# A two-layer encoder trunk on one core: feed-forward tiles in twos, transposes in longer runs, another job order

## The chip, the cores and the metric

The kernel runs on one core of a Trainium2 chip. The metric is the device time of one execution in microseconds (us). The kernel before took 728.59 us, the median of three runs (728.37 to 728.87).

A core has TensorE (matrix products, written to eight PSUM banks), VectorE, ScalarE and GpSimd (elementwise work), and SyncE, whose queue issues the transfers from memory. In the profile these are PE (its weight loads are PEld), DVE, ACT, POOL and SP.

## The reference

The input is one sequence of 256 positions, 1024 wide. Each of the two layers does, with float32 weights:

```python
ada = c_act @ w_ada[l] + b_ada[l]            # six vectors of 1024: shift, scale, gate, twice
h = rms(x, g_mix[l]) * (1.0 + sc1) + sh1
parts = split(h @ w_in[l])                    # queries, keys, values, two gates
y_a = gqa_attention(qa, ka, va) @ w_branch_a[l]      # 8 query heads, 2 key heads, 256 keys
y_b = dilated_attention(qs, kss, vs) @ w_branch_b[l] # 3 groups of 4 heads, strided windows
x = x + gt1 * ((sigmoid(ga) * y_a + sigmoid(gb) * y_b) @ w_out[l])
h2 = rms(x, g_mlp[l]) * (1.0 + sc2) + sh2
x = x + gt2 * (square(relu(h2 @ w_ff1[l])) @ w_ff2[l])   # 1024 -> 4096 -> 1024
```

Queries and keys are normalized and rotated before the attention.

## The kernel before

**Two-part numbers.** A large product is computed from operands split into a high part and a low remainder, each in the reduced float32 format that TensorE takes in one pass. A weight tile (128 x 1024, 512 KB) is loaded to a buffer `wr`; ScalarE copies it into the high half of a buffer `w`, and VectorE subtracts to make the low half (`split_next`). A product then is three passes: high by high, low by high, high by low (`mm3`, `many`).

**The first feed-forward layer.** The 4096 hidden columns are taken in eight rounds j of 512. Round 0 (`ff1_first`) has its own form. In rounds 1 to 7, `ff1(j)` handles four tiles of 128 columns, two for each half u. For a tile, `two_sums` runs eight *wide* passes: the tile's high half is the stationary operand, and the high and low parts of the activations stream through side by side, 512 columns, into one PSUM bank. Then eight *narrow* passes follow, with the tile's low half and the activations' high part, 256 columns, added to the bank's first half. ScalarE and VectorE add the bank's halves, apply the squared ReLU and split the result. Between two rounds stand the passes of the second feed-forward layer for the round before: four weight tiles of twelve wide passes each.

**Transposes.** Normalized activations, queries, keys, mixed values and attention probabilities are transposed on TensorE, 128 x 128 at a time, as `pe.transpose` against the identity (in the profile a MATMUL with `xin`, which holds the identity, and 128 columns), and copied out of PSUM by ScalarE or VectorE. In `att_a_soft`, for one step j of the grouped attention, the two key heads g come one after the other: maximum (VectorE), two exponentials with sums (ScalarE), reciprocal, two scalings (ScalarE), four transposes into a bank, a copy out.

**Order.** No engine's order is written by hand. Every operation is recorded (`Plan.record`; all instructions therefore carry line 676, where they are issued) with an estimated occupancy and latency. `Plan.due` gives each a due time, working back from TensorE's order, and `Plan.run` then plays the program forward in time: on each engine that is free, the ready operation with the earliest due time goes next, if a buffer or bank for its result can be had (`fits`). This is done in four passes, each taking its due times from the starts of the one before, and the best of the four by its own clock is issued. For TensorE the planner knows a price for changing between products that use the whole array and those that use parts of it (`CUT`, by the `cut` of an operation); a transpose counts as whole, and changing to or from one is free in its account. `plan.together()` marks operations that must follow one another without anything between; the first of them then waits for what any of them needs.

**Jobs.** TensorE's first order, from which the due times start, is the order of recording. In the mixer of a layer it is the list `seq0` or `seq1` in `CFG`: `c2` to `c5` a block of the query, key and value projection, `u` and `v` half a gate block, `a` a step of the grouped attention, `b` a step of the dilated one, `y` a part of the branch projection, `w` one tile of the modulation vectors `ada` (a 512 KB load and one VectorE reduction of 128 x 1024, nothing on TensorE). `ada_f0` and `ada_f1` say how many such tiles follow each feed-forward round. The weight tiles are loaded by SP's queue in the order in which the jobs name them.

Of the kernel before, what the change touches and what calls it, by code (L numbers as in the profile page):

```python
# [20 lines left out]
P = 128  # L21
D = 1024
S = 256
# [3 lines left out]
KT = D // P  # L27
# [6 lines left out]
CFG = dict(ahead0=1,  # L34
  post0=(5, 2, 1, 0), s2k=9, ahead=1, last="k",
  hk=2,
  ada_f0=[1, 5, 6, 1, 1, 6, 1, 4, 2], ada_f1=[4, 0, 0, 0, 0, 2, 1, 0, 0],
  seq0="a v w v w w c4 c3 w w w v a a u u w w w v a w w w w w b w w w u w v w b w w y w y w y w y".split(),
  seq1="v w w a w u a w c4 w v c3 w w w w u c5 w w w u a w a c2 w y w y y u y b w w w w b v w w w v".split())
WR = 7  # L40
NB8 = 16
WARM = 5
# [3 lines left out]
BEGIN = 20000.0  # L46
# [15 lines left out]
    shift={})  # L62
COLD = 5200.0
FILL = (6000.0, 3), (8500.0, 4)
CUT = {"row": 290.0, "col": 240.0, "rowcol": 290.0, "": 125.0}
DEEP = 3
URGE = 500.0
GIVE = 0.75
# [73 lines left out]
def pattern(z):  # L142
    return z.ap if isinstance(z, View) else z if hasattr(z, "tensor") else None
# [10 lines left out]
class Plan:  # L154
# [101 lines left out]
    def record(self, e, op, a, k):  # L256
        outs = [k["out"]] if "out" in k else [a[0]]
        outs += [z for z in (k.get("accum_out"),) if z is not None]
        ins = [z for z in list(a if "out" in k else a[1:]) + [v for n, v in k.items() if n not in ("out", "accum_out")] if pattern(z) is not None]
        if op == "tensor_tensor_reduce":  # L260
            outs.append(ins.pop())
        o = dict(e=e, op=op, a=a, k=k, w=[self.foot(z) for z in outs], r=[self.foot(z) for z in ins], i=len(self.ops))
        o["also"], o["then"], o["soon"] = [], None, self.soon and e == "SP"
        o["from"] = self.earliest
        if self.group is not None:
            self.group.append(o)
        outs, ins = [pattern(z) for z in outs], [pattern(z) for z in ins]
        o["occ"], o["lat"] = self.cost(e, op, outs, ins, k)
        o["occ"] += self.hold
        o["cut"] = ""  # L270
        if e == "PE" and op == "matmul":
            o["cut"] = self.division(outs[0], ins[0])
        o["rush"] = self.urgent and e in ("DVE", "ACT")
        from_sbuf = all(z.space == bass.MemoryType.SB for z in ins)
        o["port"] = from_sbuf and op != "reciprocal" and k.get("op") != ALU.pow and "reduce" not in op.replace("tensor_tensor_reduce", "")
        self.ops.append(o)
# [145 lines left out]
    def run(self, due):  # L422
        ops = self.ops
        n = len(ops)
        left = [len(o["need"]) for o in ops]
        ready = [o["from"] for o in ops]
        start = [None] * n
# [5 lines left out]
        dve_port, held_port, last_cut = 0.0, (0.0, 0.0), ""  # L433
# [68 lines left out]
        def taken(i):  # L502
            z = 0.0
            for name in banks[i]:
                e, end = reader.get(name, (None, 0.0))
                if e != ops[i]["e"]:
                    z = max(z, end)
            return z
# [5 lines left out]
        t = 0.0  # L514
        count = 0
        while count < n:
            moved = False
            for e in ORDERED:
                if free[e] > t:
                    continue  # L520
                w, q = wait[e], now[e]
                if then[e] is not None:
                    pick = then[e]
# [4 lines left out]
                else:  # L528
                    pick = None
                while w and w[0][0] <= t:  # L530
                    i = heapq.heappop(w)[1]
# [6 lines left out]
                held = []  # L538
                forced = pick is not None
                while q and not forced:  # L540
                    d, i = heapq.heappop(q)
                    z = taken(i)
                    if z > t:
                        heapq.heappush(ev, (z, 0, -1))
                        if e not in again:
                            again.append(e)
                    elif fits(i):
                        pick = i
                        break
                    held.append((d, i))  # L550
                    if len(held) > 40:
                        break
                if pick is None:
                    seen[e] = state[0]
                if pick is not None and e != "SP" and not forced:

                    end = t + ops[pick]["occ"]
                    for r, j in w:
                        if r < end and due[j] < due[pick] - self.patience and (r - t) < 0.5 * ops[pick]["occ"] and fits(j):
                            held.append((due[pick], pick))  # L560
                            pick = None
                            break
                    if pick is not None and rushed[e] and not ops[pick]["rush"] and called(e, pick, end):
                        held.append((due[pick], pick))
                        pick = None
# [9 lines left out]
                o = ops[pick]  # L575
                then[e] = o["then"]
                start[pick] = t
                slow = 0.0
                if e == "PE":
                    cut = o["cut"]  # L580
                    if cut != last_cut:
                        slow = CUT[cut]
                    last_cut = cut
                    if t < COLD and o["occ"] < 1000.0:
                        slow += o["occ"]
                if e == "DVE" and o["port"]:
                    if held_port[0] <= t < held_port[1]:
                        slow = held_port[1] - t
                    dve_port = t + o["occ"] + slow
                elif e == "POOL" and not o["port"]:  # L590
                    slow = max(0.0, dve_port - t - 80.0)
                elif e == "POOL" and o["port"]:

                    slow = max(0.0, dve_port - t - 80.0)
# [3 lines left out]
                if e == "SP":  # L598
                    quiet = t < 4000.0
                    b = max(pipe[0], t + (1200.0 if t < 4000.0 else 2100.0)) + o["lat"] / RATE[t < 50000.0]  # L600
# [29 lines left out]
            t = max(t, ev[0][0])  # L630
            while ev and ev[0][0] <= t:
                _, kind, i = heapq.heappop(ev)
# [47 lines left out]
def encoder(ctx: ExitStack, tc: tile.TileContext, a: dict, out: bass.AP):  # L680
# [4 lines left out]
    plan = Plan(tc, dict(sbuf=pool_of("ap"), psum=pool_of("pp", space=PSUM)))  # L685
    act, dve, pool, pe, sp = plan.lanes()
    tl = plan.tile

    def pa(name):
        return tl("psum", [P, 512], F32, "ps", 8, name)  # L690
# [4 lines left out]
    def pt(name):  # L695
        return tl("psum", [P, 512], F32, "ps", 8, name)
# [10 lines left out]
    ident, small, gc = xin[:, :P], xin[:, P : 2 * P], xin[:, 2 * P : 2 * P + 8]  # L707
# [102 lines left out]
    def weights(n=None):  # L810
        while todo and len(ready) < (n or CFG["ahead"]):
            split_next()
        return ready.pop(0)

    def weights_k(k):
        return [z.rearrange("p (k n) -> p k n", k=k) for z in weights()]
# [259 lines left out]
    def keep_pt(ps, o):  # L1076
        act.activation(o, ps, AF.Copy)
        return o
# [15 lines left out]

    def att_a_soft(l, j, sps, home):

        pts = []
        for g in range(2):
            nm = f"a{l}_{g}_{j}"
            sv = sps[j, g].rearrange("p (t n) -> p t n", t=2)  # L1100
            st = tl("sbuf", [P, 3, 2], F32, "st", 6, f"st{nm}")
            dve.tensor_reduce(out=st[:, 0, :], in_=sv, op=ALU.max, axis=AX.X, negate=True)
            pr = tl("sbuf", [P, 2, S], F32, "pr", 4, f"pr{nm}")
            for t in range(2):
                act.activation(
                    pr[:, t, :], sv[:, t, :], AF.Exp, bias=st[:, 0, t : t + 1], accum_out=st[:, 1, t : t + 1]
                )
            dve.reciprocal(st[:, 2, :], st[:, 1, :])
            for t in range(2):
                scale_p(pr[:, t, :], st[:, 2, t : t + 1], PSCALE[l])  # L1110
            tp = pt(f"t{nm}")
            for kt in range(2):
                for t in range(2):
                    pe.transpose(
                        tp[:, kt * S + t * P : kt * S + (t + 1) * P], pr[:, t, kt * P : (kt + 1) * P], ident
                    )
            pts.append(keep_pt(tp, home[:, 2 * (j % 2) + g]))
        return pts

    def att_a_out(l, T, j, pts, ops):  # L1120

# [105 lines left out]

    def two_sums(ps, wh, wl, xs, nk):  # L1230

        for k in range(nk):
            pe.matmul(ps, wh[:, k, :], xs.both(k).rearrange("p u n -> p (u n)"), start=k == 0, stop=False)
        for k in range(nk):
            pe.matmul(ps[:, :S], wl[:, k, :], xs.both(k)[:, 0], start=False, stop=k == nk - 1)

    fl = lambda z: z.rearrange("p a b -> p (a b)")

# [136 lines left out]
    def mlp(l, h2):  # L1375
# [42 lines left out]
        def ff1(j):  # L1418
            hid = hid_tiles(j)
            for u in range(2):  # L1420
                r = s2k(f"r{l}_{j}_{u}")
                for i in range(2):
                    wh, wl = weights_k(KT)
                    ps = pa(f"f{l}_{j}_{u}{i}")
                    two_sums(ps, wh, wl, h2, KT)
                    ri = r[:, i * S : (i + 1) * S]
                    act.activation(ri, ps[:, S:], AF.Copy)
                    dve.tensor_tensor(ri, ps[:, :S], ri, op=ALU.add)
                act.activation(r, r, AF.Relu)
                act.activation(r, r, AF.Square)  # L1430
                split_hid(r, *hid[u])
            return hid
# [17 lines left out]
        for j in range(1, 8):  # L1450
            hids.append(ff1(j))
            ada(ffn_ada[j])
            if j < 7:
                for i in range(4):
                    w = weights()
# [4 lines left out]
        ws = []  # L1460
# [47 lines left out]
        for c0 in halves:  # L1508
            cs = slice(c0, c0 + 256)
            acc = pb(f"gated{c0}")[:, :256]  # L1510
            for q, (j, i, w) in enumerate(ws[6:]):
                wh, wl = (gated[:, q, z, c0 - 512 : c0 - 256] for z in range(2))
# [21 lines left out]
    c_row, pick = c_in[:, :P], c_in[:, P:]  # L1534
# [102 lines left out]
    pss = {c: [pb(f"q0_{c}_{t}") for t in range(2)] for c in (0, 1, 2, 5)}  # L1637
# [42 lines left out]
    for k in range(1, KT):  # L1680
        ada(2)
        v = shg[0, 0]
# [5 lines left out]
        for pair in ((0, 1), (2, 5)) if k < KT - 1 else ((2, 5), (0, 1)):  # L1688
            w = weights(CFG["ahead0"])
            jobs = []  # L1690
            for t in range(2):
                for i, c in enumerate(pair):
                    wh, wl = (z[:, i * 512 : (i + 1) * 512] for z in w)
# [10 lines left out]
    h2 = mixer(0, hT, T)  # L1704
# [8 lines left out]
    ws = []  # L1713
    for t in range(2):
        pss = [pb(f"q1_{c}_{t}") for c in range(2)]
        for k in range(KT):
            if t == 0:
                ws.append(weights())
            for c in range(2):
                lh, ll = hT.parts(k, slice(t * P, (t + 1) * P))  # L1720
                wh, wl = (z[:, c * 512 : (c + 1) * 512] for z in ws[k])
# [3 lines left out]
    h2 = mixer(1, hT, T)  # L1725
# [99 lines left out]
```

## Time and profile before

| | |
|---|---|
| median of three runs | 728.59 us (728.37 to 728.87) |
| the profiled execution's own time | 728.5 us |
| its span, first to last instruction | 726.7 us |
| PE busy | 721.3 us, 99%, 3844 matmuls |
| DVE, ACT, POOL busy | 584.1, 467.0, 64.9 us |
| moved by DMA | 180.95 MB, mean 249 GB/s |
| granted TensorE clock | 1.00 |

Matmuls are pipelined, and the length that the profile gives one (some 0.39 us for a wide pass) runs on while the next has begun. The pace is read from one start to the next. In the timeline view neighbouring instructions of one kind form a row: its start, the time to the end of its last, what it is, and how many; what it writes stands ahead of `<-` and what it reads behind it. A transpose between wide passes splits a row of them.

### The profile page before, as it was taken

The page shows a single profiled execution, that of the slowest core. Times are in us where ns is not written, and L with a number is a line of the kernel's source. Part 1 is how long each engine was busy: PE and PEld are TensorE (multiplying, and loading weights), DVE is VectorE, ACT ScalarE, POOL GpSimd, SP SyncE. Part 2 cuts the span into 40 slices and gives each one's busy share as a digit, 9 for nine tenths or more (in the row PEclk, how much of TensorE's full clock was granted, in tenths as well). Part 3 has the DMA queues.
Part 4 walks back from the last instruction along what each step waited for, and adds up shares of the span by engine and source line. Part 5 has one row for each costly group of instructions (what it writes and reads, how often), then busy time and mean ns, then how long its engine had stood idle before and what let it go on. Part 6 is the DMA issues. An engine that isn't in the chain of part 4 may idle for free.

```text
span 726.7 us, 10619 instructions
## 1 busy us (share of the span) xinstructions
PE 721.3 (99%) x3844; PEld 599.1 (82%) x3844; DVE 584.1 (80%) x911; ACT 467.0 (64%) x791; POOL 64.9 (9%) x60
## 2 busy tenths in 40 slices
PE   9999999999999999999999999999999999999998
PEld 7787887788888888888887888778888888888887
DVE  6999999999999878683799788797889965566543
ACT  6669679875657765663475946858846856556540
POOL 1007540000000050000003011010000000000000
PEclk9999999999999999999999999999999999999999
DMA  8997669996499988684556777858456965686201
GB/s 350 407 406 246 203 202 326 355 356 211 144 343 400 380 321 308 252 298 146 203 161 225 246 276 262 297 175 285 142 207 217 379 242 172 210 286 179 83 0 59
DMA packets 50868, 180.95 MB, mean 249 GB/s; under 512 B 5728, under 2 KB 6784, under 8 KB 50816
## 3 DMA queue, kind: packets, MB, share of 16 engines
q1 hardware_dynamic: 50816, 180.28, 70.6%
q8 instruction: 30, 0.49, 0.3%
q14 instruction: 22, 0.18, 0.1%
HBM read 178.66 MB, written 1.06 MB: 247 GB/s over the span
## 4 chain that ended last, share of the span: by engine, by line
PE 96%; ACT 1%; DVE 1%; DMA 1%; issue 0%; POOL 0%; SPq 0%; DVEq 0%
PE ps L676 96%; DMA xin<-in_x 1%; ACT pr L676 0%; ACT s2k L676 0%; ACT w L676 0%; DVE s2k L676 0%; POOL ss L676 0%; DVE w L676 0%; ACT v L676 0%; DVE st L676 0%; DVE xin L676 0%; SPq L676 0%; DVE ss L676 0%; DVEq L676 0%; DVE shg L676 0%
## 5 line engine op out<-in xcount | busy, mean ns | idle before, releaser
L676 DVE TENSOR_TENSOR w<-wr,w 128x1024 fp32r<-128x1024 f32 x234 | 281.4, 1224 | 43.4 <-ACT w L676 42.5
L676 ACT ACTIVATE w<-wr 128x1024 fp32r<-128x1024 f32 x234 | 240.4, 1058 | 60.7 <-PE ps L676 39.2
L676 PE MATMUL ps<-w,hT 128*128 128x512 f32 x1032 | 250.3, 396 | 0.2 <-DVE s2k L676 0.2
L676 PEld LDWEIGHTS ps<-w,hT 128*128 128x128 f32 x1032 | 190.1, 188 | 41.6 <-issue 1.4
L676 PE MATMUL ps<-w,hid 128*128 128x512 f32 (+1 forms) x780 | 176.0, 385 | 0.0
L676 PEld LDWEIGHTS ps<-w,hid 128*128 128x128 f32 x780 | 143.1, 188 | 28.3
L676 PE MATMUL ps<-hT,w 128*128 128x256 f32 (+1 forms) x896 | 159.1, 337 | 0.0
L676 PEld LDWEIGHTS ps<-hT,w 128*128 128x128 f32 x896 | 139.2, 189 | 19.3
L676 DVE CUSTOM_DVE_ANT_0 s2k<-wr,c_act 128x1024 bf16<-128x1024 f32 x96 | 116.6, 1222 | 4.5 <-DMA wr<-in_w_ada 4.5
L676 ACT ACTIVATE s2k<-ps 128x256 f32<-128x256 f32 (+3 forms) x108 | 44.8, 444 | 78.3 <-PE ps L676 78.1
L676 PE MATMUL ps<-w,mT 128*128 128x512 f32 x192 | 45.7, 393 | 0.0
L676 DVE TENSOR_TENSOR s2k<-ps,s2k 128x256 f32<-128x256 f32 x56 | 23.1, 419 | 26.0 <-ACT s2k L676 25.9
L676 ACT ACTIVATE s2k<-s2k 128x512 f32<-128x512 f32 (+1 forms) x62 | 38.5, 623 | 8.3 <-DVE s2k L676 7.4
L676 PEld LDWEIGHTS ps<-w,mT 128*128 128x128 f32 x192 | 35.5, 188 | 7.2 <-DVE mT L676 0.2
L676 POOL TENSOR_TENSOR rstd<-rstd,half 128x8 f32<-128x8 f32 (+1 forms) x20 | 31.0, 1554 | 100.0 <-DVE rstd L676 99.7
L676 DVE TENSOR_TENSOR hid<-s2k,hid 128x512 fp32r<-128x512 f32 x28 | 19.2, 689 | 24.1 <-ACT hid L676 24.0
L676 ACT ACTIVATE pr<-pr,st 128x256 f32<-128x256 f32 (+1 forms) x64 | 32.7, 563 | 2.7 <-DVE st L676 2.7
L676 POOL TENSOR_TENSOR ss<-ss,half 128x1 f32<-128x1 f32 x8 | 5.8, 730 | 257.4 <-DVE ss L676 257.4
L676 PE MATMUL ps<-xin,s2k 128*128 128x128 f32 x180 | 26.9, 273 | 0.7 <-ACT s2k L676 0.7
L676 PEld LDWEIGHTS ps<-xin,s2k 128*128 128x128 f32 x180 | 21.7, 140 | 6.9 <-ACT s2k L676 1.4
L676 PE MATMUL ps<-w,oa 128*128 128x512 f32 x96 | 24.0, 397 | 0.0
L676 DVE TENSOR_TENSOR s2k<-ps,gtb 128x512 f32<-128x512 f32 (+1 forms) x18 | 11.7, 658 | 15.0 <-PE ps L676 15.0
(106 smaller groups left out, 508.0 us busy)
## 6 DMA issues: line engine op xcount, KB each, us to landing
wr<-in_w_ff SPq DMA_DIRECT2D x120, 512.0 KB, 5.0
wr<-in_w_ada SPq DMA_DIRECT2D x96, 512.0 KB, 5.3
wr<-in_w_gate SPq DMA_DIRECT2D x32, 512.0 KB, 5.4
wr<-in_w_qkv SPq DMA_DIRECT2D x24, 512.0 KB, 4.9
wr<-in_w_x SPq DMA_DIRECT2D x16, 512.0 KB, 5.6
wr<-in_w_out SPq DMA_DIRECT2D x16, 512.0 KB, 5.1
wr<-in_w_y SPq DMA_DIRECT2D x8, 512.0 KB, 6.5
wr<-in_w_ba SPq DMA_DIRECT2D x8, 512.0 KB, 6.1
```

Of the source, the lines that this page charges most:

```text
L676: getattr(self.real[o["e"]], o["op"])(*map(real, o["a"]), **{n: real(z) for n, z in o["k"].items()})
```

## The change

1. `two_sums` takes a list of banks and tiles. `ff1(j)` calls it once for each half u with both tiles: sixteen wide passes, then sixteen narrow ones, instead of eight and eight, twice. Both banks and both weight tiles are held until the end.
2. Transposes get a `cut` of their own, `"t"`: going to them is free in the planner's account, going back to a whole-array product costs 55 ns (`LEAVE`).
3. When TensorE's next operation by due time is of another kind than the last one, the planner looks among the 40 ready operations that are due first for one of the last kind: due at most 1000 ns later if the last was a transpose or used parts of the array (`LINGER`), 300 ns if it was an ordinary product (`SHY`). If there is one, it goes first. This holds from 20 us on.
4. `att_a_soft` records the softmax of both key heads first, and then the eight transposes into two banks under `plan.together()`, and the two copies behind them.
5. `seq0`, `seq1`, `ada_f0` and `ada_f1` have another order. Layer 0's list keeps the first jobs nearly as they are and moves the last gate job behind both dilated steps; layer 1's begins with a gate job and a projection block.

```diff
-  ada_f0=[1, 5, 6, 1, 1, 6, 1, 4, 2], ada_f1=[4, 0, 0, 0, 0, 2, 1, 0, 0],
-  seq0="a v w v w w c4 c3 w w w v a a u u w w w v a w w w w w b w w w u w v w b w w y w y w y w y".split(),
-  seq1="v w w a w u a w c4 w v c3 w w w w u c5 w w w u a w a c2 w y w y y u y b w w w w b v w w w v".split())
+  ada_f0=[3, 1, 8, 2, 1, 6, 2, 4, 2], ada_f1=[2, 0, 0, 0, 0, 0, 0, 0, 0],
+  seq0="w a v w v w w c3 c4 w w v a a w u u w w v a w w w w w b w v b w w w w w w w u y w y y y w w".split(),
+  seq1="u w c4 v a w w w w w u a c3 w v a c5 u w w w w w w c2 w a w y y y y u b b v v w w w w w w w v w".split())
...
-CUT = {"row": 290.0, "col": 240.0, "rowcol": 290.0, "": 125.0}
+CUT = {"row": 290.0, "col": 240.0, "rowcol": 290.0, "": 125.0, "t": 0.0}
+LEAVE = 55.0
+LINGER = 1000.0
+SHY = 300.0
...
+        if e == "PE" and op == "transpose":
+            o["cut"] = "t"
...
+                if e == "PE" and pick is not None and not forced and t > BEGIN and ops[pick]["cut"] != last_cut:
+                    more = LINGER if last_cut else SHY
+                    for d, i in sorted(q)[:40]:
+                        if d > due[pick] + more:
+                            break
+                        if ops[i]["cut"] == last_cut and fits(i):
+                            q.remove((d, i))
+                            heapq.heapify(q)
+                            held.append((due[pick], pick))
+                            pick = i
+                            break
...
-                        slow = CUT[cut]
+                        slow = LEAVE if last_cut == "t" and not cut else CUT[cut]
...
-            tp = pt(f"t{nm}")
-            for kt in range(2):
-                for t in range(2):
-                    pe.transpose(
-                        tp[:, kt * S + t * P : kt * S + (t + 1) * P], pr[:, t, kt * P : (kt + 1) * P], ident
-                    )
-            pts.append(keep_pt(tp, home[:, 2 * (j % 2) + g]))
-        return pts
+            prs.append(pr)
+        tps = [pt(f"ta{l}_{g}_{j}") for g in range(2)]
+        with plan.together():
+            for g in range(2):
+                for kt in range(2):
+                    for t in range(2):
+                        pe.transpose(
+                            tps[g][:, kt * S + t * P : kt * S + (t + 1) * P], prs[g][:, t, kt * P : (kt + 1) * P], ident
+                        )
+        return [keep_pt(tps[g], home[:, 2 * (j % 2) + g]) for g in range(2)]
...
-    def two_sums(ps, wh, wl, xs, nk):
-
-        for k in range(nk):
-            pe.matmul(ps, wh[:, k, :], xs.both(k).rearrange("p u n -> p (u n)"), start=k == 0, stop=False)
-        for k in range(nk):
-            pe.matmul(ps[:, :S], wl[:, k, :], xs.both(k)[:, 0], start=False, stop=k == nk - 1)
+    def two_sums(pss, ws, xs, nk):
+
+        for ps, (wh, _) in zip(pss, ws):
+            for k in range(nk):
+                pe.matmul(ps, wh[:, k, :], xs.both(k).rearrange("p u n -> p (u n)"), start=k == 0, stop=False)
+        for ps, (_, wl) in zip(pss, ws):
+            for k in range(nk):
+                pe.matmul(ps[:, :S], wl[:, k, :], xs.both(k)[:, 0], start=False, stop=k == nk - 1)
...
-                for i in range(2):
-                    wh, wl = weights_k(KT)
-                    ps = pa(f"f{l}_{j}_{u}{i}")
-                    two_sums(ps, wh, wl, h2, KT)
+                ws = [weights_k(KT) for _ in range(2)]
+                pss = [pa(f"f{l}_{j}_{u}{i}") for i in range(2)]
+                two_sums(pss, ws, h2, KT)
+                for i, ps in enumerate(pss):
```

More of the change, by code (lines that the diff above doesn't have):

```diff
@@ L36 @@
   hk=2,
-  ada_f0=[1, 5, 6, 1, 1, 6, 1, 4, 2], ada_f1=[4, 0, 0, 0, 0, 2, 1, 0, 0],
-  seq0="a v w v w w c4 c3 w w w v a a u u w w w v a w w w w w b w w w u w v w b w w y w y w y w y".split(),
-  seq1="v w w a w u a w c4 w v c3 w w w w u c5 w w w u a w a c2 w y w y y u y b w w w w b v w w w v".split())
+  ada_f0=[3, 1, 8, 2, 1, 6, 2, 4, 2], ada_f1=[2, 0, 0, 0, 0, 0, 0, 0, 0],
+  seq0="w a v w v w w c3 c4 w w v a a w u u w w v a w w w w w b w v b w w w w w w w u y w y y y w w".split(),
+  seq1="u w c4 v a w w w w w u a c3 w v a c5 u w w w w w w c2 w a w y y y y u b b v w w w w w w w w v w".split())
 WR = 7
@@ L1095, in att_a_soft @@
     def att_a_soft(l, j, sps, home):
-        pts = []
+        prs = []
         for g in range(2):
```

## The prediction

> **What bounds the kernel now.** I read the page's busy shares and slices first, then its waits, then TensorE's timeline piece by piece.
>
> ```profile
> PE 721.3 (99%) x3844; PEld 599.1 (82%) x3844; DVE 584.1 (80%) x911; ACT 467.0 (64%) x791; POOL 64.9 (9%) x60
> ...
> PEclk9999999999999999999999999999999999999999
> ```
>
> ```profile
> PEld ps L676 <- issue: 5.0, 17, 0.4
> PEld ps L676 <- ACT s2k L676: 2.3, 3, 0.9
> PEld ps L676 <- ACT pr L676: 1.4, 3, 0.7
> ...
> PEld ps L676 <- DVE w L676: 0.4, 1, 0.4
> ```
>
> TensorE is busy for 99% of the span at full clock, and nothing holds it long: its weight loads wait 5.0 us for issue and 2.3 us on the largest engine row. No matmul is added or removed. The gain can only come from what consecutive matmuls cost beyond their steady pace, and from the few waits. That pace is read from start to start in the timeline (columns: start us, length us, what, count).
>
> ```profile
> 246.31 11.31 PE L676 MATMUL ps<-hT,w 128*128 128x512 f32 x64
> 257.45 11.07 PE L676 MATMUL ps<-w,hid 128*128 128x512 f32 x48
> 268.36 11.31 PE L676 MATMUL ps<-hT,w 128*128 128x512 f32 x64
> ...
> 334.52 5.72 PE L676 MATMUL ps<-hT,w 128*128 128x512 f32 x32
> ...
> 701.35 20.82 PE L676 MATMUL ps<-w,hid 128*128 128x512 f32 x108
> 722.01 1.60 PE L676 MATMUL ps<-gated,hid 128*128 128x256 f32 x12
> ```
>
> ```profile
> L676 PE MATMUL ps<-gated,hid 128*128 128x256 f32 x12 | 1.6, 283 | 0.0
> ```
>
> One round of the feed-forward (one j) takes (334.52 − 246.31) / 4 = 22.053 us. By the code it holds 80 wide passes (32 in the x64, 48 in the x48) and 32 narrow ones, in 4 groups of 8 wide, 8 narrow. A narrow pass takes n = (1.60 − 0.283) / 11 = 0.120 us. The x108 piece holds 72 wide and 36 narrow and follows a narrow group. Let e be what it costs to go from narrow back to wide: 722.01 − 701.35 = 20.66 = 72 w + 36 n + e, and 22.053 = 80 w + 32 n + 4 e. These give w = 0.227 us and **e = 0.019 us**; reading errors of 0.01 us move e by some 0.005.
>
> **Part 1, tiles in twos.** Two tiles' wide passes run together, then their narrow ones: 28 groups per layer become 14, so over both layers 28 returns go, 28 × 0.019 = **−0.53 us**. It is on TensorE, so on the path. Unknown is whether the return costs more after 16 narrow passes than after 8. If it doubles, the gain is 0; if not, 0.53. I take 0.53, because inside a group the narrow passes keep their pace (the 12 at the end give the same 0.120), so nothing visible builds up. What moves besides: the second tile's high half is needed 8 narrow passes (0.96 us) earlier, and the first tile's low half 8 wide ones (1.8 us) later. Covers: the weights. The loads' waits above show one wait for a low half, 0.4 us, in the whole run, and this stage is where it would be tightest:
>
> ```profile
> 204.00:226.00 22.00, 22.00 (x114) 18.78 (x113) 21.62 (x34) 14.26 (x21) 0.00 (x0) 1.00 0.98 379
> 226.00:248.00 22.00, 22.00 (x114) 18.82 (x113) 21.88 (x29) 18.03 (x25) 0.00 (x0) 1.00 1.01 396
> ```
>
> ```profile
> ACT w L676 <- PE ps L676: 39.2, 25, 3.7
> ```
>
> VectorE is 98% to 99% busy and the DMA engines are full there (shares 0.98 and 1.01), yet TensorE never pauses; and the copies of the weights' high halves wait 39.2 us in all for TensorE to give back a buffer or a bank, so they are ahead of it. I cost it at nothing; were the lead gone, each of 28 pairs could lose up to 0.96 us. The results leave later: both banks of a pair are drained after its narrow passes, while the next pair writes two others; the 10.91 us of second-layer passes between rounds hide the rest.
>
> **Part 2, transposes in longer runs.** The transposes stand in some 75 runs behind the opening, from 64.06 to 679.17 us.
>
> ```profile
> 64.06 0.60 PE L676 MATMUL ps<-xin,s2k 128*128 128x128 f32 x4
> ...
> 170.99 0.60 PE L676 MATMUL ps<-xin,s2k 128*128 128x128 f32 x4
> 171.35 11.17 PE L676 MATMUL ps<-w,mT 128*128 128x512 f32 x48
> 182.36 1.04 PE L676 MATMUL ps<-xin,s2k 128*128 128x128 f32 x8
> ...
> 193.46 1.04 PE L676 MATMUL ps<-xin,s2k 128*128 128x128 f32 x8
> 194.25 7.10 PE L676 MATMUL ps<-w,hT 128*128 128x512 f32 x30
> 201.19 0.60 PE L676 MATMUL ps<-xin,s2k 128*128 128x128 f32 x4
> ...
> 679.17 0.27 PE L676 MATMUL ps<-xin,gcol 128*8 128x128 f32 x1
> ```
>
> The 8 give one transpose: (1.04 − 0.27) / 7 = 0.110 us. Four with 48 wide passes behind them should take 0.44 + 48 × 0.2268 = 11.33 and take 11.37: 0.04 us lost by one run. Eight with 30 behind: 0.88 + 6.80 = 7.68 against 7.73, 0.05. Between 182.36 and 193.46 (8 and 45, in two rows not shown) it is 0.015. So a run costs some **0.035 us, whether of 4 or of 8**. Now the scattered ones of the grouped attention's softmax, first pair of layer 1:
>
> ```profile
> 402.41 0.27 PE L676 MATMUL ps<-xin,pr 128*128 128x128 f32 x1
> 402.44 0.48 PE L676 MATMUL ps<-w,hT 128*128 128x512 f32 x1
> 402.75 0.49 PE L676 MATMUL ps<-xin,pr 128*128 128x128 f32 x3
> ...
> 408.25 0.49 PE L676 MATMUL ps<-xin,pr 128*128 128x128 f32 x3
> 408.50 10.02 PE L676 MATMUL ps<-w,hT 128*128 128x512 f32 x43
> 418.36 0.27 PE L676 MATMUL ps<-xin,gcol 128*8 128x128 f32 x1
> ```
>
> Seven runs, 16 transposes and 62 wide passes: 1.75 + 14.06 = 15.82 against 15.95, so 0.13 lost. The edit makes each softmax step an unbroken run of 8: two runs, 0.07. Gain 0.06. Likewise the three other scattered places (layer 0 at 89 and 114 us, layer 1 at 465) give 0.04, 0.07 and 0.13 by the same count, 0.30 together. Elsewhere the planner's new look-ahead joins runs whose due times lie within 1000 ns, some four wide passes. I count 19 such gaps of at most five passes; between 499.93 and 506.10 us two of them cost 0.05, so 0.025 each:
>
> ```profile
> 499.93 0.38 PE L676 MATMUL ps<-xin,pr 128*128 128x128 f32 x2
> ...
> 506.10 0.38 PE L676 MATMUL ps<-xin,pr 128*128 128x128 f32 x2
> ```
>
> All 19 would be 0.48; a gap closes only where the later transpose is ready, so I take half, 0.25. Sum **−0.55 us**, bounds 0 (none join) and −0.8.
>
> The Trainium skill, TensorEngine Tiling (Array Packing), Tiling Modes, says that changing the tiling mode drains TensorE, and changing the tile alone does not. Transposes and wide passes both use the whole 128 by 128 array, so by that rule a run would cost nothing and this term would be 0; the trace's 0.04 and 0.05 us speak against it.
>
> What the softmax edit adds is a wait: the first transpose of a step now waits for both key heads' probabilities. Behind it in TensorE's order stands whatever the planner put there, and the copy out of the bank and later the weighted sums wait for it.
>
> **Part 3, the job order.** Gate, projection and attention jobs change places; of the 94 modulation tiles behind the opening, 25 instead of 24 lie in layer 0's mixer, 29 instead of 27 in its feed-forward, 24 instead of 22 in layer 1's mixer, 2 instead of 7 in its feed-forward. Each brings one 512 KB load on SP's queue and 1.22 us of VectorE, and moves past weight loads in that queue. All of it is off TensorE; the FFN rows above bound it: even at 0.98 DMA share TensorE did not wait. What the order can change on TensorE are the pauses:
>
> ```profile
> 396.20 0.71 PE L676 MATMUL ps<-w,hT 128*128 128x512 f32 x2
> 396.90 0.30 PE L676 MATMUL ps<-xin,s2k 128*128 128x128 f32 x1
> ...
> 463.81 1.07 PE L676 MATMUL ps<-w,hT 128*128 128x512 f32 x4
> 465.20 0.33 PE L676 MATMUL ps<-xin,pr 128*128 128x128 f32 x1 [0.32 <-ACT pr L676]
> ```
>
> Four wide passes need 0.91 us and took 1.39: 0.48 lost in layer 1's second softmax pair. Two need 0.45 and took 0.70: 0.25 lost at its first projections. In the new order layer 1 starts with a gate job and a projection ahead of the first attention step, and another gate job stands by the later ones, so TensorE has other work. I take the first pause whole and half of the second, **−0.60 us**; bounds −1.1 (both go, and one of the visits to the split array, which the scores at 398 and 458 us make, joins another) and the loss in the third rival.
>
> **The sum.** −0.53 − 0.55 − 0.60 = −1.68. The profiled execution took 728.5 us around its span of 726.7, the runs' median 728.59, so the two agree within 0.1: 728.59 − 1.68 = **726.9**. Opening and closing writes stay.
>
> **The rivals.**
> *Runs and groups cost by the instruction, not by the change of kind.* If a transpose or a narrow pass itself delays the wide ones behind it, regrouping returns nothing. For it: four and eight transposes cost alike only within 0.03 us, single ones less. Against: the equations above, and 0.13 for seven runs against 0.07. Then only part 3 stays: 728.0. If only the transposes' term fails, 727.5. Either is no change. The second is also what the Trainium skill's rule of TensorEngine Tiling (Array Packing), Tiling Modes, would give.
>
> *The search found more.* Its order also decides how often TensorE visits the split array, and what the ends of the layers wait for. A visit:
>
> ```profile
> 398.06 2.00 PE L676 MATMUL ps<-ka,qk 64*128 64x256 f32 x16
> 399.99 2.58 PE L676 MATMUL ps<-w,hT 128*128 128x512 f32 x10
> 402.41 0.27 PE L676 MATMUL ps<-xin,pr 128*128 128x128 f32 x1
> ```
>
> The ten passes behind it take 2.42 instead of 2.27, so 0.15 on the way out alone. Two visits joined and all transposes gathered: about −3.0, 725.6. Against: the attention steps mostly keep their distances.
>
> *The joined softmax starves TensorE.* Its run of 8 waits for the second head's chain on ScalarE:
>
> ```profile
> L676 ACT ACTIVATE pr<-pr,st x64: 492/580/622, 87.5 to 507.3; 128x256 f32<-128x256 f32 x32, 128x384 f32<-128x384 f32 x32
> L676 ACT ACTIVATE pr<-ps,st x32: 462/476/523, 85.7 to 465.4; 128x256 f32<-128x256 f32 x32
> L676 ACT ACTIVATION_READ_ACCUMULATOR pr<-ps,st x32: 192/208/256, 86.1 to 465.8; 128x1 f32 x32
> ```
>
> Two exponentials, two sums, two scalings: 2 × (0.476 + 0.208 + 0.54) = 2.4 us. At 465 us TensorE already waits for exactly these. If no other work fills the time there, both steps of that pair lose 2.4 each: parts 1 and 2 alone, −1.1, and 4.8 give +3.7, 732.3; one step alone +1.3, 729.9. It ends slower than before from 1.1 us of waiting on. Against: the planner knows the wait, the weighted sums are due much later, and the new order puts more work by these steps.
>
> **How the numbers follow.** Forecast 0.46, its own range 726.2 to 727.7; more found 0.20; costs by instruction or no gain of the transposes 0.20; starved 0.14 (732.3 when both steps lose, 729.9 with one). About 0.2%, 1.46 us, is what a measurement of this kernel can tell from no change: faster lies below 727.13, slower above 730.05. The forecast gives 0.31 faster, 0.15 same; more found 0.20 and 0; the flat cases 0.02 and 0.18; starved 0.02 same and 0.12 slower. Faster 0.53, same 0.35, slower 0.12. The range leaves out a tenth on each side: 725.2 to 729.8, which holds both flat cases and a single starved step.
>
> **What would show it.** Feed-forward rounds of 21.99 to 22.02 us instead of 22.05; 16 unbroken transposes of the probabilities per pair, in runs of 8; fewer runs in all, below 60; no pause marked before the probabilities' transposes of layer 1; busy time and counts unchanged on all engines. Wrong it is if TensorE shows new idle time behind ScalarE's probabilities or the weights, if rounds stay at 22.05, or if a run's cost grows with its length.

## The result and the profile after

The changed kernel takes 727.32 us (median of 13 runs, 726.64 to 727.67) against 728.46 for the kernel before, measured beside it: a ratio of 0.9982, 95% interval 0.9974 to 0.9991. Run again beside the last experiments below it took 727.32 against 728.89, ratio 0.9977 (0.9968 to 0.9986). So it is faster by about 0.2%, 1.1 to 1.6 us. The prediction said 726.9, within 725.2 to 729.8.

Busy shares on the page and the loads' waits, of the changed kernel:

```profile
PE 720.1 (99%) x3844; PEld 599.6 (83%) x3844; DVE 584.6 (81%) x911; ACT 466.9 (64%) x791; POOL 65.6 (9%) x60
...
PEclk9999999999999999999999999999999999999999
```

```profile
PEld ps L692 <- issue: 5.0, 17, 0.4
PEld ps L692 <- ACT s2k L692: 2.6, 5, 0.9
PEld ps L692 <- DVE s2k L692: 1.7, 5, 0.7
...
PEld ps L692 <- ACT pr L692: 0.6, 2, 0.4
```

The counts of instructions are the same on every engine. In the waits of the weight loads, the one for the probabilities (`pr`) fell from 1.4 to 0.6 us, and the one for VectorE's results in `s2k`, the normalized queries and keys among them, rose from 1.2 to 1.7. TensorE's timeline, feed-forward rounds:

```profile
268.60 11.27 PE L692 MATMUL ps<-hT,w 128*128 128x512 f32 x64
279.71 11.07 PE L692 MATMUL ps<-w,hid 128*128 128x512 f32 x48
290.62 11.27 PE L692 MATMUL ps<-hT,w 128*128 128x512 f32 x64
...
334.64 10.55 PE L692 MATMUL ps<-hT,w 128*128 128x512 f32 x58
```

A round takes (334.64 − 268.60) / 3 = 22.013 us instead of 22.053. Layer 1's grouped attention, the stretch with the seven runs and the pause:

```profile
421.09 1.04 PE L692 MATMUL ps<-xin,pr 128*128 128x128 f32 x8
421.88 3.44 PE L692 MATMUL ps<-w,hT 128*128 128x512 f32 x14
425.16 1.04 PE L692 MATMUL ps<-xin,pr 128*128 128x128 f32 x8
425.95 15.00 PE L692 MATMUL ps<-w,hT 128*128 128x512 f32 x65
440.79 0.60 PE L692 MATMUL ps<-xin,s2k 128*128 128x128 f32 x4
441.32 2.00 PE L692 MATMUL ps<-ka,qk 64*128 64x256 f32 x16
443.25 0.66 PE L692 MATMUL ps<-xin,s2k 128*128 128x128 f32 x4
443.66 4.14 PE L692 MATMUL ps<-w,hT 128*128 128x512 f32 x17
447.64 1.04 PE L692 MATMUL ps<-xin,pr 128*128 128x128 f32 x8
448.43 23.62 PE L692 MATMUL ps<-w,hT 128*128 128x512 f32 x103
471.89 1.04 PE L692 MATMUL ps<-xin,pr 128*128 128x128 f32 x8
```

Each softmax step is one unbroken run of eight, and no idle time is marked before any. The two pieces of four beside the scores (441.32) will matter below.

**A balance by stage.** A single execution says more than the medians here, because its stages can be compared one by one. For each stage I took the time from its first matmul to the next stage's first, and subtracted what its passes take at their steady pace (wide 0.2267, narrow 0.1199, transposes 0.1092 us) and the small products of the attention as they ran. What is left is lost. Of it I call *pause* what a single start-to-start step took beyond the usual for its pair of kinds (238 ns wide to wide, 318 for the first wide one behind a transpose, 341 behind the split array, and so on, counted from 8 ns over that), and *changes* the rest. The split between the two is a convention, the sum is not. In us, for the profiled executions; the opening, up to the first transposes at some 64 us, is left out:

| kernel | pauses, mixers 0 + 1 | changes, mixers 0 + 1 | lost in both feed-forward stages | sum | transpose runs in the mixers |
|---|---|---|---|---|---|
| before | 0.08 + 1.08 | 1.93 + 2.16 | 1.40 | 6.65 | 72 |
| changed | 0.56 + 0.39 | 1.83 + 1.32 | 0.92 | 5.02 | 49 |
| changed, again | 0.51 + 0.43 | 1.83 + 1.34 | 0.92 | 5.03 | 49 |
| tiles in twos alone | 0.11 + 1.06 | 1.93 + 2.07 | 0.88 | 6.05 | 72 |
| gathering alone | 0.23 + 1.09 | 1.69 + 1.92 | 1.57 | 6.51 | 50 |
| new lists alone | 1.04 + 0.62 | 2.03 + 1.56 | 1.38 | 6.64 | 67 |
| changed, old lists | 0.19 + 1.00 | 1.69 + 1.85 | 1.06 | 5.78 | 50 |
| joined softmax alone | 0.53 + 0.86 | 1.84 + 1.92 | 1.37 | 6.51 | 59 |
| changed, not joined | 1.36 + 0.50 | 1.98 + 1.49 | 0.92 | 6.25 | 57 |
| changed, no look-ahead | 0.94 + 0.63 | 1.80 + 1.47 | 0.89 | 5.73 | 54 |
| changed, old first list | 0.20 + 0.41 | 1.73 + 1.34 | 0.99 | 4.68 | 48 |
| changed, in fours | 0.48 + 0.39 | 1.81 + 1.43 | 0.72 | 4.83 | 49 |

The change takes 6.65 − 5.02 = 1.63 us out of these stages: 0.48 in the feed-forward stages, 0.94 in changes and 0.21 in pauses of the mixers. The last is a gain of 0.69 in layer 1 and a loss of 0.48 in layer 0.

How far the split depends on its rule shows in one case. The first transpose directly behind the split array holds TensorE for 166 ns instead of 109, and the table counts that as a pause. It happens once in the kernel before and four times in the changed one, three of them in layer 1; counted as changes instead, the 0.94 and 0.21 would be 0.77 and 0.38.

### The profile page after: what moved, and what is told of

It is laid out like the page before. It is cut to its first block, busy times and chain, and to the rows that moved or that the text cites. A ratio compares the mean times of both kernels' runs of the same rounds, so it can differ in the third digit from the quotient of the medians.

```text
span 725.0 us, 10593 instructions
## 1 busy us (share of the span) xinstructions
PE 720.1 (99%) x3844; PEld 599.6 (83%) x3844; DVE 584.6 (81%) x911; ACT 466.9 (64%) x791; POOL 65.6 (9%) x60
## 3 DMA queue, kind: packets, MB, share of 16 engines
HBM read 178.66 MB, written 1.06 MB: 248 GB/s over the span
## 4 chain that ended last, share of the span: by engine, by line
PE 92%; DVE 4%; DMA 1%; ACT 1%; issue 1%; POOL 0%; SPq 0%; ACTq 0%; DVEq 0%
PE ps L692 92%; DVE s2k L692 2%; DVE w L692 1%; DMA wr<-in_w_x 1%; DMA xin<-in_x 1%; ACT s2k L692 0%; ACT hT L692 0%; POOL ss L692 0%; ACT w L692 0%; DVE shg L692 0%; DVE w20wx L692 0%; DVE hT L692 0%; DVE xT L692 0%; DVE rstd L692 0%; DVE xin L692 0%
## 5 line engine op out<-in xcount | busy, mean ns | idle before, releaser
L692 PE MATMUL ps<-w,hT 128*128 128x512 f32 x1032 | 246.0, 394 | 0.3 <-DVE s2k L692 0.3
L692 PE MATMUL ps<-hT,w 128*128 128x512 f32 (+1 forms) x896 | 158.6, 337 | 0.0
L692 POOL TENSOR_TENSOR s2k<-s2k,tabs 128x256 f32<-128x256 f32 (+1 forms) x20 | 18.0, 919 | 52.7 <-ACT s2k L692 52.5
```

Of the source, the lines that this page charges most:

```text
L692: getattr(self.real[o["e"]], o["op"])(*map(real, o["a"]), **{n: real(z) for n, z in o["k"].items()})
```

## The experiments

All were timed in five rounds beside the kernel before, four at a time on one chip.

**Tiles in twos alone.** The kernel before with the new `two_sums` and `ff1`.

> The kernel before with the feed-forward tiles in twos and nothing else. Theory (a return from narrow to wide passes costs 0.019 us whatever the length of the narrow run): rounds of 22.01 us instead of 22.05, 28 x 0.019 = 0.53 us less in all, about 727.9. Rival (the cost goes with each narrow pass): rounds of 22.05 and 728.5. Second rival (the plan made anew around it shifts something in the mixers): rounds of 22.01, and a total that does not follow them.

728.3 against 728.96, ratio 0.9991 (0.9982 to 0.9999). The feed-forward stages lose 0.52 us less, 0.26 in each layer, as the theory has it; the mixers keep their runs and pauses.

**Four and four.** The test of the mechanism the other way round, on the kernel before:

```diff
-        for k in range(nk):
-            pe.matmul(ps, wh[:, k, :], ...)          # eight wide
-        for k in range(nk):
-            pe.matmul(ps[:, :S], wl[:, k, :], ...)   # eight narrow
+        for h in range(0, nk, 4):
+            for k in range(h, h + 4): ...            # four wide
+            for k in range(h, h + 4): ...            # four narrow
```

> The kernel before with each tile's eight wide and eight narrow passes in two portions: four wide, four narrow, four wide, four narrow. No pass is added; the returns from narrow to wide double, 56 more. Theory (0.019 us a return): rounds of 22.05 + 4 x 0.019 = 22.13 us, and 56 x 0.019 = 1.06 us more in all, 0.15% over the kernel before. Rival (cost by the narrow pass): rounds of 22.05, no change. Between them: if what a return costs is filled up by the narrow passes before it and four are too few to fill it, rounds between the two.

729.97 against 728.71, ratio 1.0017 (1.0009 to 1.0026). TensorE's timeline:

```profile
269.09 11.36 PE L676 MATMUL ps<-hT,w 128*128 128x512 f32 x64
280.29 11.09 PE L676 MATMUL ps<-w,hid 128*128 128x512 f32 x48
...
313.35 11.36 PE L676 MATMUL ps<-hT,w 128*128 128x512 f32 x64
```

(313.35 − 269.09) / 2 = 22.13, the number expected. A return costs 0.019 us after four narrow passes as after eight. The feed-forward stages lose 0.95 us more in all, of the 1.06 expected; the rest of the median's 1.26 does not come from them.

**In fours.** The changed kernel with all four tiles of a round in one `two_sums`:

```diff
-            for u in range(2):
-                ws = [weights_k(KT) for _ in range(2)]
-                pss = [pa(f"f{l}_{j}_{u}{i}") for i in range(2)]
-                two_sums(pss, ws, h2, KT)
+            ws = [weights_k(KT) for _ in range(4)]
+            pss = [pa(f"f{l}_{j}_{i}") for i in range(4)]
+            two_sums(pss, ws, h2, KT)
```

> The changed kernel with all four tiles of a round together: 32 wide passes, then 32 narrow. Theory (one return is saved per round, 14 x 0.019 = 0.27 us, and the banks just suffice: four for the second layer's sums, four here): rounds of 21.99 us, 0.27 us below the changed kernel, 0.19% below the one before. Rival (no bank is left for a transpose or for the next round's first tile, and the result leaves late): TensorE waits between rounds, and rounds of 22.05 or more.

727.26 against 728.71, ratio 0.9977 (0.9968 to 0.9986).

```profile
269.18 11.25 PE L692 MATMUL ps<-hT,w 128*128 128x512 f32 x64
280.27 11.07 PE L692 MATMUL ps<-w,hid 128*128 128x512 f32 x48
...
313.17 11.25 PE L692 MATMUL ps<-hT,w 128*128 128x512 f32 x64
```

(313.17 − 269.18) / 2 = 21.995. With 8, 4, 2 and 1 returns in a round it takes 22.13, 22.053, 22.013 and 21.995 us: 0.019, 0.020 and 0.018 for each return less, where the rounding of the rows can move each by some 0.005. The banks suffice. The whole time can't tell this kernel from the changed one.

**Gathering alone.** The kernel before with the look-ahead, the price for leaving transposes, and the joined softmax.

> The kernel before with the planner's look-ahead for operations of the same kind, the price for leaving transposes, and the eight joined transposes of each softmax step; job order and tiles as before. Theory (a run of transposes costs 0.035 us whatever its length, the pauses stay): about 55 runs instead of some 75, 0.55 us less, 727.9, gained in both mixers. Rival (the joined softmax makes TensorE wait in the old order, which has no other work at 465 us): the pause there grows from 0.5 us to 1 or 2 and the total is 728.5 to 730.

728.91 against 728.96, ratio 0.9998 (0.9989 to 1.0007): no difference. The runs fell from 72 to 50 and the changes by 0.48 us, as the theory has it. But pauses in the mixers grew by 0.16. In layer 1 they only moved: the one at 465 us, which the rival expected to grow, is gone, the one at 396 us doubled, and one at 424 us is new.

```profile
393.61 3.11 PE L692 MATMUL ps<-w,hT 128*128 128x512 f32 x13
396.88 0.63 PE L692 MATMUL ps<-xin,s2k 128*128 128x128 f32 x4 [0.16 <-DVE s2k L692]
...
420.65 3.56 PE L692 MATMUL ps<-w,hT 128*128 128x512 f32 x15
424.28 0.66 PE L692 MATMUL ps<-xin,s2k 128*128 128x128 f32 x4
```

Thirteen wide passes take 2.95 us and took 3.27, and fifteen take 3.40 and took 3.63: before both runs of transposes TensorE waits for VectorE's `s2k`. The growth itself is in layer 0, 0.15 us, nearly all before and in the run of four at 171 us. Another 0.17 is lost in the feed-forward stages, half of it in a pause at 559 us.

**Joined softmax alone.** Only the edit of `att_a_soft`, on the kernel before.

> The kernel before with the eight transposes of a softmax step joined, and nothing else. Theory (scattered runs become one each): 12 to 15 runs fewer in the two mixers, 0.3 us less, 0.04% below before. Rival (the joined run waits for ScalarE's second chain, and the old order has nothing to fill it with): the pause at 465 us grows from 0.5 us towards 2.4, and the total is 0.1 to 0.3% above before.

728.73 against 728.89, ratio 0.9998 (0.9989 to 1.0007). Thirteen runs fewer and 0.33 us less in changes, as the theory has it. The feared wait did not come at its place; the old pause at 465 us went:

```profile
461.52 6.01 PE L676 MATMUL ps<-w,hT 128*128 128x512 f32 x25
467.37 1.06 PE L676 MATMUL ps<-xin,pr 128*128 128x128 f32 x8
468.19 1.18 PE L676 MATMUL ps<-w,hT 128*128 128x512 f32 x4
469.20 1.04 PE L676 MATMUL ps<-xin,pr 128*128 128x128 f32 x8
```

25 wide passes behind a visit to the split array should take 5.67 + 0.15 and took 5.85. The planner, which now may not begin the step early, puts seven more wide passes ahead of it. A new pause of 0.25 us came at 425.6 us, before other transposes. And 0.44 us was lost anew at the end of layer 0's mixer, where the loads waited for the new activations `hT`:

```profile
PEld ps L676 <- ACT hT L676: 0.6, 1, 0.6
```

**The new lists alone.**

> The kernel before with the new job lists alone. Theory (the order takes the pauses at 396 and 465 us away by itself): layer 1's mixer 0.6 us shorter, about 727.9. Rival (the order was found for the new planner and fits it alone): the pauses move and the total is 728.5 to 730; layer 0's mixer, which was 0.44 us longer in the changed kernel, would be longer here too if the order is the cause of that.

729.29 against 728.96, ratio 1.0003 (0.9994 to 1.0011): no gain. Layer 1's mixer lost 1.06 us less: 0.46 in pauses, which the theory had at 0.6, and 0.60 in changes, which it did not have. Layer 0's lost 1.07 more, 0.44 of it in the same wait for `hT`, most of the rest in small pauses before transposes. The rival is right on the total, the theory on layer 1.

**The changed kernel with the old lists.**

> The changed kernel with the old job lists: tiles in twos and gathered transposes. Theory (the parts add up): 0.53 + 0.55 less than before, about 727.4, and layer 0's mixer not 0.44 us longer. Rival (look-ahead and order belong together): no better than 728.0, with a pause before the probabilities' transposes of layer 1.

728.25 against 728.96, ratio 0.9993 (0.9984 to 1.0002), less than the sum expected; layer 0's mixer indeed is not longer than before. The pause that the rival expects is there, but at 423 us before queries and keys (0.38 us), not before probabilities.

**Not joined.** The changed kernel with the old `att_a_soft`.

> The changed kernel with the old softmax step: four transposes for each key head as they become ready, not eight joined; the planner's look-ahead stays. Theory (joining is what removes the scattered runs of the probabilities): some 12 to 15 more runs in the mixers, 0.035 us each, 0.3 to 0.5 us more than the changed kernel, about 0.10% below the one before. Rival (the look-ahead alone gathers them, and joining only adds waiting): runs within 3 of the changed kernel's and the time the same or less.

728.77 against 728.71, ratio 1.0002 (0.9993 to 1.0011): the whole gain is gone, 1.2 us in the balance. Eight more runs cost 0.32 in changes; 0.91 are pauses, among them the wait for `hT` once more:

```profile
195.15 1.04 PE L692 MATMUL ps<-xin,s2k 128*128 128x128 f32 x8
195.79 1.16 ACT L692 ACTIVATE s2k<-ps,shg 128x128 f32<-128x128 f32 x3 [1.86 <-PE ps L692]
...
195.94 1.17 PE L692 MATMUL ps<-w,hT 128*128 128x512 f32 x4
...
197.31 1.42 PE L692 MATMUL ps<-w,hT 128*128 128x512 f32 x5 [0.20 <-ACT hT L692]
```

Behind the last eight transposes TensorE has four wide passes left that don't need them; the chain that makes new activations from them takes longer. In the changed kernel six loads go first there, and the wait is 0.16 us and hidden:

```profile
194.51 1.22 PEld L692 LDWEIGHTS ps<-w,hT 128*128 128x128 f32 x6
...
195.90 2.14 PEld L692 LDWEIGHTS ps<-w,hT 128*128 128x128 f32 x10 [0.16 <-ACT hT L692]
```

**No look-ahead.** The changed kernel without `LINGER`, `SHY` and `LEAVE`.

> The changed kernel without the planner's look-ahead and without its price for leaving transposes; joined softmax transposes, tiles in twos and new lists stay. Theory (the look-ahead joins about half of the 19 small gaps): eight to twelve more runs than the changed kernel's 54, 0.2 to 0.4 us more, and no new pauses. Rival (the lists were found with the look-ahead, and without it layer 0's mixer pauses at its end, as it did under the new lists alone and without joining): a pause of 0.3 us or more at about 197 us, 1 us more in all.

728.04 against 728.89, ratio 0.9988 (0.9979 to 0.9996). Five runs more, 0.12 us in changes, and 0.62 in pauses, 0.44 of them at 196 us: the rival's pause.

**The old first list.** The changed kernel with layer 0's old `seq0`.

> The changed kernel with layer 0's old job list; the one modulation tile that this list has less goes to the first feed-forward round (4 instead of 3), all else as changed. Theory (the new list of layer 0 causes the 0.38 us that its mixer lost, by transposes that wait for VectorE, and the new list of layer 1 brings its gain without it): layer 0's mixer back to what gathering alone gave it there, 0.5 us shorter than in the changed kernel, layer 1's mixer still 1.4 us shorter than before; 0.5 us below the changed kernel in all, 0.22% below the one before. Rival (the two lists are bound to each other through the modulation tiles and buffers): layer 1's mixer loses as much as layer 0's wins.

727.2 against 728.71, ratio 0.9977 (0.9968 to 0.9987). Layer 0's mixer loses 0.46 us less than in the changed kernel, layer 1's loses the same (1.76 against 1.71). The first list is thus the cause of layer 0's loss, though the medians alone can't tell these two kernels apart. The pauses lie at four places of the changed kernel, 66, 104, 109 and 173 us, 0.1 to 0.2 us each. Two rows of VectorE and one of the weight loads at 104 us:

```profile
102.44 1.21 DVE L692 CUSTOM_DVE_ANT_0 s2k<-wr,c_act 128x1024 bf16<-128x1024 f32 x1
...
103.59 0.68 DVE L692 TENSOR_TENSOR s2k<-s2k,rstd 128x512 f32<-128x512 f32 x1
...
104.32 0.42 PEld L692 LDWEIGHTS ps<-xin,s2k 128*128 128x128 f32 x4 [0.23 <-DVE s2k L692]
```

A modulation tile's reduction stands ahead of the product whose result the transposes wait for. But TensorE's order differs too: in the changed kernel one wide pass lies between the transposes of the probabilities and these, with the old first list five:

```profile
103.14 1.04 PE L692 MATMUL ps<-xin,pr 128*128 128x128 f32 x8
103.93 0.48 PE L692 MATMUL ps<-w,hT 128*128 128x512 f32 x1
```

```profile
102.60 1.04 PE L692 MATMUL ps<-xin,pr 128*128 128x128 f32 x8
103.39 1.40 PE L692 MATMUL ps<-w,hT 128*128 128x512 f32 x5
104.63 0.61 PE L692 MATMUL ps<-xin,s2k 128*128 128x128 f32 x4
```

Which of the two makes the wait, and whether the list's extra modulation tile or its swapped blocks bring it about, was not separated.

**The changed kernel again.**

> The changed kernel once more, on the chip of the runs beside it. Its first profiled execution was 0.5 us faster than the median of its runs. Theory (the difference lies in the first 60 us, where TensorE waits for loads that land a little earlier or later in each execution): mixers and feed-forward stages within 0.1 us of the first profile's, the opening up to 0.6 us longer; ratio to before 0.998. Rival (the pauses of layer 0's mixer come and go): that stage differs by 0.3 us or more.

Every later stage repeats within 0.06 us (the table); the opening, counted from TensorE's first matmul, took 63.38 instead of 62.70. Most of that lies in one row, 39.48 us to the next here and 38.96 in the first profile:

```profile
19.15 39.23 PE L692 MATMUL ps<-w,hT 128*128 128x512 f32 x168
58.63 5.74 PE L692 MATMUL ps<-w,hT 128*128 128x512 f32 x24 [0.25 <-DVE s2k L692]
```

```profile
18.99 38.69 PE L692 MATMUL ps<-w,hT 128*128 128x512 f32 x168
57.95 5.96 PE L692 MATMUL ps<-w,hT 128*128 128x512 f32 x25 [0.27 <-DVE s2k L692]
```

The theory holds on the place; that the loads' landing is the reason was not shown.

**Old first list and fours.**

> Layer 0's old job list and all four tiles of a round together, the rest as changed: the two variants that took 0.5 us and 0.27 us off. Theory (they add up): layer 0's mixer 0.5 us and the rounds 0.02 us each shorter than in the changed kernel, 0.75 us in all, 0.27% below the kernel before. Rival (four banks a round hold up what the old list needs): one of the two is lost, 0.20 to 0.23%.

726.97 against 728.89, ratio 0.9973 (0.9961 to 0.9984); 4.43 us lost in the balance, 0.59 less than in the changed kernel: 0.49 in layer 0's mixer and 0.11 in the feed-forward stages, with layer 1's mixer the same. So the mixer's half of the theory holds, and of the 0.27 us expected of the rounds 0.11 arrived. It is the fastest of all by the balance; the medians, 726.97 and 727.32 on one chip, point the same way, but their intervals overlap.

## Why the prediction was right, and where not

**Part 1 (−0.53)** was right in size and mechanism: 0.52 alone, 0.48 in the changed kernel (where layer 0's stage gave 0.21 of its 0.27). The unknown that it named, whether the return grows with the narrow run, is settled by the series of rounds: it does not, between 4 and 32 passes. The steps from start to start in the changed kernel's feed-forward show why: the five wide passes behind a narrow run take 27 ns over their pace together, the first two narrow ones 7 ns under it, and all others keep it, however many there are. The cover held: the loads' waits no longer name a low half `w`.

**Part 2 (−0.55)** had the right size in changes, 0.48 alone, but "0.035 whether of 4 or of 8" was only roughly so: 22 runs less saved 0.48, or 0.022 a run, because runs that one wide pass parts cost less than two full ones; the prediction's own seven scattered runs cost 0.13, or 0.019 each. The step that failed is that the planner's delays were priced at nothing: with the old lists the pauses and the feed-forward stages took 0.33 of it back, so gathering alone moved the time by nothing that could be measured. The Trainium skill, TensorEngine Tiling (Array Packing), Tiling Modes, has TensorE drain when the tiling mode changes and not when only the tile does. Transposes and wide passes are both 128*128 in these rows, so by that rule alone a run would cost nothing; the 0.48 us that came out of the changes when runs were joined disagree.

**Part 3 (−0.60)** named the right places: layer 1's pauses fell by 0.69. Two things were left out. Layer 0's pauses grew by 0.48, and with its old list put back 0.36 of that is gone. The step that failed is that I took TensorE's calm in the densest feed-forward stage as proof that the new order costs nothing elsewhere; the weights came in time in layer 0's mixer too, but chains whose result is used at once did not, and their waits were priced at nothing. (The count of 94 modulation tiles is wrong as well: the four stages' numbers make 80 of 96, and the other 16 run in the opening. Nothing hangs on it.) And layer 1's list saved 0.60 in changes alone (2.16 to 1.56), which stood in the prediction only as a bound. Part of it can be seen in the rows above: transposes now stand directly beside the scores. Behind the visit at 441.32, its four transposes and 17 wide passes took 447.64 − 443.25 = 4.39 us for 0.44 + 3.85, so 0.10 lost for leaving the split array and leaving the transposes together; the prediction's rows give 0.15 and 0.035 for the two apart.

**The sum (−1.68)** came to −1.63 in the profiled stages, through errors that cancel: −0.48, −0.94, −0.21 instead of −0.53, −0.55, −0.60. The terms were added as if independent, and they are not. Alone the three parts give 0.60, 0.14 and 0.01 in the balance, 0.75 in all; together 1.63. Savings in changes nearly add up (0.48 by gathering and 0.50 by the lists make 0.98, against 0.94 together). Pauses do not: gathering alone adds 0.16 and the lists alone 0.50, and both together take 0.21 off. The median's gain, 1.14 us beside the first run and 1.57 beside the second, is less certain than the balance because the opening varies by 0.7 us.

**The rivals.** Cost by the instruction is ruled out for narrow passes by the series of rounds, and for transposes by the changes, which fell by 0.48 us with the same 296 of them. The starved softmax is ruled out where it was expected: joining alone removed the pause at 465 us. What slowed kernels here instead was a wait that no rival of the prediction had priced: the end of layer 0's mixer, 0.44 us in four variants. In all four, the fifth pass behind the last eight transposes comes late, where the kernel before and the changed one have six to run first; why their plans leave only four stays open.

## What to carry to other kernels

On an engine that is busy 99% of the time, subtract the steady pace of each kind of instruction stage by stage: what is left, here 6.65 us of 727 behind the opening, is what reordering those passes can win. It splits into changes of kind, whose savings nearly added up here, and pauses, whose did not. The new lists gained nothing without the planner's new rules, and one of the two cost time even with them; so try each list and each rule on its own, since the best kernel here kept one new list and dropped the other. Cover has to be checked for each consumer: weights that come in time say nothing of a chain whose result is used at once.

## What the runs showed of the hardware

Going from 512-column to 256-column passes and back costs some 0.019 us whatever number of narrow passes lies between (4, 8, 16 or 32). The first 63 us of the changed kernel took 62.70 and 63.38 us in two executions, while each of its later stages repeated within 0.06 us.
